# An encoder kernel: the latent heads' scores as three part products, and a new order of the work beside the heads

## The chip, the cores and the metric

The kernel runs on one core of a Trainium2 chip. Times are device microseconds from start to end of one execution. The core's engines run side by side, each through its own list of instructions in order: TensorE (PE; its weight loads are shown as PEld), VectorE (DVE), ScalarE (ACT), GpSimd (POOL) and SyncE (SP), which here only issues DMA transfers. Engines wait for each other through semaphores.

## The reference

Two layers of an encoder for 512 tokens of width 1024, float32. Each layer mixes tokens with three groups of heads, then attends to 256 memory tokens, then runs a gated feed-forward part. What matters here:

```python
a_q, a_k, a_v, b_cq, b_ckv, b_kr, c_q, c_k, c_v = split(rmsnorm(x, g_mix_pre[l]) @ w_in[l])
# latent heads: 4 heads, 64 plain + 32 rotated channels for q and k, 64 for v
qb = (rmsnorm(b_cq, mla_q_norm_g[l]) @ mla_w_q_up[l]).reshape(B, S, 4, 96)
qb = concat([qb[..., :64], rope(qb[..., 64:], positions)])
kvb = (rmsnorm(b_ckv, mla_kv_norm_g[l]) @ mla_w_kv_up[l]).reshape(B, S, 4, 128)
kb = concat([kvb[..., :64], broadcast(rope(b_kr, positions))])
s = einsum('bqhd,bshd->bhqs', qb, kb) / sqrt(96)         # the latent heads' scores
o_b = einsum('bhqs,bshd->bqhd', softmax(s), kvb[..., 64:])
o_a = diff_attention(...)   # 4 heads;  o_c = swa_attention(...)  # 8 heads, window of 128
x = x + rmsnorm(concat([o_a, o_b, o_c]) @ w_out[l], g_mix_post[l])
k, v = split(rmsnorm(mem, g_x_mem[l]) @ w_xkv[l])        # cross attention's keys, values
x = x + rmsnorm(attend(rmsnorm(x, g_x_pre[l]) @ w_xq[l], k, v) @ w_xo[l], g_x_post[l])
gate, up = split(rmsnorm(x, g_ffn_pre[l]) @ w_ffn_in[l])
x = x + rmsnorm((silu(gate) * up) @ w_ffn_out[l], g_ffn_post[l])
```

## The kernel before, in words

**Products.** A float32 operand is split into a high part (ScalarE casts it to float32r, L103) and a low part (VectorE subtracts the high part from it, L104). A product is then three float32r matmuls into one accumulator: high x high, high x low, low x high (`mm3`, L150 to L152). Two things stay plain float32: transposes (a matmul with the identity, L183, L416, L783) and the scores of the latent heads (L801). A plain float32 matmul shows as two records in the trace.

**The mix phase of a layer** is a list of 64 units in the order of the heads: 16 of the differential heads (units 0 to 15), 32 of the windowed heads (16 to 47), 16 of the latent heads (48 to 63). A unit goes through stages: scores (`score`), softmax (`soft`: VectorE finds the row's maximum, ScalarE exponentiates), transposes of the softmax (L416), splits of them (`ph`, `pl`), products with the values (L589, L590; accumulator `av`) and the eviction. At each step t of the list one stage of several units is emitted.

**Filling.** Between units, a generator `fill` emits other tensor work, as much per step as `FILL_PLAN` allows. Its order is: the rest of the projections into the heads; then the pieces that the string `FILL_ORDER` lists, one letter per piece; then the keys' rest, the values, and, from unit 48 on, the output projection (`out_first`, `early`, `out_late`). The letters are q, the windowed heads' second half of q; u, the latent heads' up-projection; m, the norm of the memory; k, the cross attention's keys (`make_xK`). The tile framework then schedules each engine's list from priorities and dependences, so the list that an engine runs can differ from the text's order.

**The up-projection** (`mla_up`) loads two weights, splits them, and goes over four tiles of 128 tokens. In `products` it multiplies the normed latents (`latT`) with the weights, copies, rotates (VectorE, L763 to L774) and writes the values `mV` (high on ScalarE, L424, low on VectorE, L425). In `transposed` it transposes q and k of four heads (L783) and ScalarE writes them, scaled, as float32 into `qT` and `kT` (L784). A letter u emits the transposes of the tile before and the products of the next.

**The memory's norm** (`mem_norm`) works on two tiles of 128 memory tokens, each in two halves: SyncE loads them into buffers named o, of which there are two (L1059); ScalarE squares and sums (L202); GpSimd makes the factor (L206, L207); VectorE scales in place (L223); TensorE transposes (L183); ScalarE and VectorE write high and low parts (`memTh`, `memTl`). Two letters m are one tile.

**Buffers.** Two accumulators (PSUM) for each of the names mm, sc, at, av; two staging buffers `st` for weights; eight pairs of split weights (`wh`, `wl`); named slots (Q0, Q1, D, E and others) that stages of a layer use one after the other. x0 to x3 hold the residual, 512 tokens; in the mix phase they hold the windowed heads' q (`SQ`: x0 and x1 for units 16 to 31, x2 and x3 for units 32 to 47), and the residual's tiles are loaded again at L1324.

SyncE issues all loads and stores in one queue, in order: one that waits for its buffer holds all behind it.

## Time and profile before

| what | us |
|---|---|
| median of 3 runs | 1575.53 (1573.16 to 1575.6) |
| profiled execution | 1577.2 |
| its span from first to last instruction | 1575.4 |
| TensorE matmuls / weight loads busy | 1539.2 / 1312.4 |
| VectorE, ScalarE, GpSimd busy | 980.2, 799.5, 93.7 |

Busy time is summed over instructions; weight loads lie beside matmuls, and the end of a matmul's record reaches over the start of the next. The trace's clock of TensorE is the granted share of full speed.

### The profile page before, as it was taken

The numbers are of one execution on the slowest core, as the hardware profiler recorded it, in microseconds if no ns is written. First come the engines' busy times: TensorE is split into PE (matmuls) and PEld (weight loads), VectorE is DVE, ScalarE is ACT, GpSimd is POOL, SyncE is SP. The second block draws the span as 40 slices with busy tenths as digits, with TensorE's granted clock in tenths as the row PEclk, the third lists the DMA queues.
The fourth block names the chain that finished last, engine by engine and source line by source line (L and its number), as shares of the span: only waits on it lengthen the run. The fifth ranks groups of instructions, "written<-read, shape, count | busy, mean of one in ns | idle before, by whom it ended". The sixth has DMA issues, their size and how long they took to land. (4 is left out here: it accounts for less than half of the span.)

```text
span 1575.4 us, 21922 instructions
## 1 busy us (share of the span) xinstructions
PE 1539.2 (98%) x8225; PEld 1312.4 (83%) x8225; DVE 980.2 (62%) x1927; ACT 799.5 (51%) x1741; POOL 93.7 (6%) x196
## 2 busy tenths in 40 slices
PE   6998999999999999999999999999999999999998
PEld 6987987899888888888888878778888888888886
DVE  6898877765653454454566988857546444445544
ACT  4588889544543233222356788875444532222321
POOL 2200000200100000000130000002002000000000
PEclk9999999999999999999999999999999999999999
DMA  5532551241243323232236135513303423233221
GB/s 179 161 95 88 188 164 56 81 161 54 81 134 109 105 84 104 81 116 98 89 125 148 51 125 177 167 41 107 127 36 110 144 81 107 80 108 107 80 81 54
DMA packets 130299, 168.69 MB, mean 107 GB/s; under 512 B 21776, under 2 KB 100752, under 8 KB 129424
## 3 DMA queue, kind: packets, MB, share of 16 engines
q1 hardware_dynamic: 130192, 167.28, 33.2%
q8 instruction: 65, 1.06, 0.3%
q14 instruction: 42, 0.34, 0.1%
HBM read 150.88 MB, written 10.09 MB: 102 GB/s over the span
## 5 line engine op out<-in xcount | busy, mean ns | idle before, releaser
L104 DVE TENSOR_TENSOR wl<-st,wh 128x512 fp32r<-128x512 f32 (+1 forms) x406 | 273.4, 686 | 245.1 <-ACT wh L103 244.4
L103 ACT CAST wh<-st 128x512 fp32r<-128x512 f32 (+1 forms) x406 | 243.7, 616 | 308.7 <-PE ps_mm L151 130.4
L152 PE MATMUL ps_mm<-hfh,wl 128*128 128x512 f32 (+1 forms) x384 | 142.8, 372 | 2.1 <-DVE wl L104 2.1
L150 PE MATMUL ps_av<-hfh,wh 128*128 128x512 f32 (+1 forms) x384 | 142.9, 372 | 0.0
L152 PE MATMUL ps_av<-hfh,wl 128*128 128x512 f32 (+1 forms) x384 | 142.6, 371 | 0.0
L150 PE MATMUL ps_mm<-hfh,wh 128*128 128x512 f32 (+1 forms) x384 | 142.6, 371 | 0.0
L151 PE MATMUL ps_mm<-hfl,wh 128*128 128x512 f32 (+1 forms) x384 | 142.6, 371 | 0.0
L151 PE MATMUL ps_av<-hfl,wh 128*128 128x512 f32 (+1 forms) x384 | 142.6, 371 | 0.0
L150 PE MATMUL ps_sc<-dwh,f 128*128 128x512 f32 x320 | 124.7, 390 | 0.0
L151 PE MATMUL ps_sc<-dwl,f 128*128 128x512 f32 x320 | 124.5, 389 | 0.0
L152 PE MATMUL ps_sc<-dwh,f 128*128 128x512 f32 x320 | 124.5, 389 | 0.0
L103 ACT CAST dwh<-st 128x1024 fp32r<-128x1024 f32 x40 | 40.1, 1050 | 157.5 <-PE ps_sc L152 153.6
L104 DVE TENSOR_TENSOR pl<-ps_at,ph 128x512 fp32r<-128x512 f32 (+1 forms) x128 | 82.7, 654 | 24.5 <-ACT ph L103 23.4
L152 PEld LDWEIGHTS ps_mm<-hfh,wl 128*128 128x128 f32 x384 | 72.3, 188 | 14.9 <-DVE wl L104 2.5
L151 PEld LDWEIGHTS ps_mm<-hfl,wh 128*128 128x128 f32 x384 | 72.4, 189 | 12.5
L152 PEld LDWEIGHTS ps_av<-hfh,wl 128*128 128x128 f32 x384 | 72.3, 188 | 12.5
L150 PEld LDWEIGHTS ps_mm<-hfh,wh 128*128 128x128 f32 x384 | 72.3, 188 | 12.5
L151 PEld LDWEIGHTS ps_av<-hfl,wh 128*128 128x128 f32 x384 | 72.2, 188 | 12.5
L150 PEld LDWEIGHTS ps_av<-hfh,wh 128*128 128x128 f32 x384 | 72.3, 188 | 12.3
L103 ACT CAST ph<-ps_at 128x512 fp32r<-128x512 f32 (+1 forms) x128 | 70.4, 561 | 23.9 <-PE ps_at L416 22.9
L206 POOL TENSOR_SCALAR rpost<-rpostss 128x1 f32<-128x1 f32 x24 | 11.9, 496 | 1173.1 <-ACT hTh L202 703.7
L416 PE MATMUL ps_at<-ident,e 128*128 128x128 f32 x480 | 77.2, 275 | 3.7 <-DVE memTl L104 2.1
(363 smaller groups left out, 3849.6 us busy)
## 6 DMA issues: line engine op xcount, KB each, us to landing
st<-in_w_ffn_in SPq DMA_DIRECT2D x44, 1024.0 KB, 4.9
st<-in_w_ffn_out SPq DMA_DIRECT2D x22, 1024.0 KB, 4.8
st<-in_w_xkv SPq DMA_DIRECT2D x16, 1024.0 KB, 5.4
st<-in_w_out SPq DMA_DIRECT2D x16, 512.0 KB, 5.2
st<-in_w_xq SPq DMA_DIRECT2D x8, 1024.0 KB, 5.3
st<-in_w_xo SPq DMA_DIRECT2D x8, 1024.0 KB, 5.0
st<-in_w_in SPq DMA_DIRECT2D x12, 512.0 KB, 3.9
q<-stg SPq DMA_DIRECT2D x48, 128.0 KB, 2.3
```

The source lines that it names most:

```text
L103: cast = nc.scalar.copy(hi, src)
L104: nc.vector.tensor_tensor(out=lo, in0=src, in1=hi.bitcast(F32), op=ALU.subtract)
L150: nc.tensor.matmul(ps, lhsT=lh, rhs=rh, start=first, stop=False)
L151: nc.tensor.matmul(ps, lhsT=lh, rhs=rl, start=False, stop=False)
L152: nc.tensor.matmul(ps, lhsT=ll, rhs=rh, start=False, stop=last)
L206: nc.gpsimd.tensor_scalar(out=r, in0=ms[:, 0:1], scalar1=ms[:, 1:2], scalar2=EPS, op0=ALU.add, op1=ALU.add)
L416: nc.tensor.transpose(pt[:, c * P:(c + 1) * P], e[:, k * P:(k + 1) * P], ident)
```

## The change

The scores of the latent heads become `mm3`, so `qT` and `kT` are each written in a high and a low part. The q part is scaled while it is written, so its low part is a multiply and subtract (two VectorE instructions, for heads 0, 1 and for heads 2, 3, into the tiles x0 and x1); the high parts are in the slots Q0 and Q1, the low part of k is in slot E. The string FILL_ORDER now also lists the values (v), and three of four tiles of the up-projection come behind the keys. At the second u the generator holds until step 31, so that the slots which units 16 to 31 read are free. The values' accumulators, staging and products are unchanged.

```diff
--- before.py
+++ after.py
@@ -38,7 +38,7 @@
 TMP_BUFS = {"e": 5, "ph": 2, "pl": 2, "o": 2, "c": 2, "m": 3}
 PS_BUFS = {"mm": 2, "sc": 2, "at": 2, "av": 2}
 NORM = {"swa": ("act", "dve"), "mla": ("act", "act")}
-FILL_ORDER = "qqummummukkkuu"
+FILL_ORDER = "qqummmmkkkkkkkkuvuuvuvv"
 FILL_PLAN = ((16, 2.5), (32, 2.2), (48, 1.6), (64, 0.8))
 FILL_STEP = 0.4
 LAG = (3, 4, 3)
@@ -741,11 +741,13 @@
                 lambda b, k: cV[:, k, 2 * b:2 * b + 2, :].rearrange("p b d -> p (b d)"), [end])
 
 
-        def mla_up(qT, kT, mV):
+        def mla_up(mla):
             st = stage(((0, 0, 0, mla_w_q_up[l].rearrange("(k p) n -> p k n", p=P)),), 2, 384)
             uq = unit(st)
             st = stage(((0, 0, 0, mla_w_kv_up[l].unsqueeze(1)),), 1, S)
             ukv = unit(st)
+
+            mV = mla["V"]
 
             def products(i):
                 t0, t1 = i * P, (i + 1) * P
@@ -776,12 +778,23 @@
                 return qn, kn
 
             def transposed(i, qn, kn):
+                qT, kT = mla["qT"], mla["kT"]
                 t0, t1 = i * P, (i + 1) * P
-                for n, t, sc in ((qn, qT, 96.0 ** -0.5), (kn, kT, 1.0)):
+                for n in (qn, kn):
                     pt = psum("at")
                     for h in range(4):
                         nc.tensor.transpose(pt[0:96, h * P:(h + 1) * P], n[:, h, :], ident)
-                    nc.scalar.mul(t[:, :, t0:t1], pt[0:96].rearrange("p (h t) -> p h t", h=4), sc)
+                    ptv = pt[0:96].rearrange("p (h t) -> p h t", h=4)
+                    if n is kn:
+                        split(kT[0][:, :, t0:t1], kT[1][:, :, t0:t1], ptv)
+                        continue
+                    sc = 96.0 ** -0.5
+                    hi = qT[0][:, :, t0:t1]
+                    nc.scalar.mul(hi, ptv, sc)
+                    for j in range(2):
+                        nc.vector.scalar_tensor_tensor(
+                            out=qT[1][j][:, :, t0:t1], in0=ptv[:, 2 * j:2 * j + 2], scalar=sc,
+                            in1=hi[:, 2 * j:2 * j + 2].bitcast(F32), op0=ALU.mult, op1=ALU.subtract)
 
             pend = None
             for i in range(NT + 1):
@@ -798,8 +811,9 @@
                 if a == 0:
                     u["nm"], u["sm"] = small(2, "mnm"), small(2, "msm")
                 ps = u["s"][a] = psum("sc")
-                nc.tensor.matmul(ps, lhsT=mla["qT"][:, h, i * P:(i + 1) * P], rhs=mla["kT"][:, h, :],
-                                 start=True, stop=True)
+                (qh, ql), k = mla["q"](h), mla["k"](h)
+                t_ = slice(i * P, (i + 1) * P)
+                mm3(ps, qh[:, t_], ql[:, t_], *k, True, True)
                 nc.vector.tensor_reduce(out=u["nm"][:, a:a + 1], in_=ps, axis=AX.X, op=ALU.max, negate=True)
 
             def soft(u, a, hi_):
@@ -813,7 +827,7 @@
 
             return chunk_units(
                 score, soft, [[((hh, i), (hh, i + 1), 0, NT) for i in (0, 2)] for hh in range(2)],
-                lambda hh, k: mla["mV"][:, k, c, 2 * hh:2 * hh + 2, :].rearrange("p b d -> p (b d)"),
+                lambda hh, k: mla["V"][:, k, c, 2 * hh:2 * hh + 2, :].rearrange("p b d -> p (b d)"),
                 [chunk_out(lambda: mdst(2 + c))])
 
 
@@ -873,22 +887,26 @@
                     head.settle()
                 yield
             qs = in_swa_q(1)
-            mla["qT"] = slot("Q0", [96, 4, S], F32, "qT")
-            mla["kT"] = slot("Q1", [96, 4, S], F32, "kT")
-            mla["mV"] = slot("D", [P, NT, 2, 4, 64], F32R, "mV")
-            ups = mla_up(mla["qT"], mla["kT"], mla["mV"])
             memT, mem_gen = mem_norm(l)
             xk = make_xK(l, memT)
-            steps = {"u": ups, "q": qs, "m": mem_gen, "k": xk}
+            steps = {"q": qs, "m": mem_gen, "k": xk, "v": make_xV(l, memT)}
             for g in FILL_ORDER:
+                if g == "u" and "k" not in mla and "u" in steps:
+                    yield 31
+                    qT = slot("Q0", [96, 4, S], F32R, "qTh"), [xp.tile([96, 2, S], F32R, tag=f"x{j}", name=f"qTl{j}")
+                                                               for j in range(2)]
+                    kT = slot("Q1", [96, 4, S], F32R, "kTh"), slot("E", [96, 4, S], F32R, "kTl")
+                    mla.update(qT=qT, kT=kT, q=lambda h: (qT[0][:, h], qT[1][h // 2][:, h % 2]),
+                               k=lambda h: (kT[0][:, h], kT[1][:, h]))
+                elif g == "u" and "u" not in steps:
+                    mla["V"] = slot("D", [P, NT, 2, 4, 64], F32R, "mV")
+                    steps["u"] = mla_up(mla)
                 next(steps[g])
                 yield
-            run_all(qs, mem_gen, ups)
+            run_all(*steps.values())
             mla["ready"] = True
-            yield from xk
             acc = slot("Sq", [P, NT, 512], F32, "acc")
             accs = state["acc"] = [acc[:, i, :] for i in range(NT)]
-            yield from make_xV(l, memT)
             yield 48 + most
             yield from out_first(w_out[l], mT, accs)
             early()
```

TensorE's list in layer 0 around the memory's second tile, first in the kernel before (L183 with `o` are the memory's transposes; `latT` and L783 belong to the up-projection; `memTh` to the keys):

```order
L183 MATMUL ps_at<-ident,o 128x128 x8
L416 MATMUL ps_at<-ident,e 128x128 x4
L589 MATMUL ps_av<-ph,KScV 128x256
L783 MATMUL ps_at<-ident,m 96x128 x8
L590 MATMUL ps_av<-pl,KScV 128x256
L589 MATMUL ps_av<-ph,KScV 128x256
L590 MATMUL ps_av<-pl,KScV 128x256
L705 MATMUL ps_sc<-KScV,SQ_555 128x256
L706 MATMUL ps_sc<-KScV,SQ_555 128x256
L705 MATMUL ps_sc<-KScV,SQ_554 128x384
L706 MATMUL ps_sc<-KScV,SQ_554 128x384
L150 MATMUL ps_mm<-wh,latT 128x384
```

The list goes on with eight more products of `latT`, the memory's other eight transposes in two groups of four, and eight transposes of L783. The same place in the changed kernel, up to the first products of the keys:

```order
L183 MATMUL ps_at<-ident,o 128x128 x8
L416 MATMUL ps_at<-ident,e 128x128 x4
L589 MATMUL ps_av<-ph,KScV 128x256
L590 MATMUL ps_av<-pl,KScV 128x256
L589 MATMUL ps_av<-ph,KScV 128x256
L590 MATMUL ps_av<-pl,KScV 128x256
L705 MATMUL ps_sc<-KScV,SQ_555 128x256
L706 MATMUL ps_sc<-KScV,SQ_555 128x256
L183 MATMUL ps_at<-ident,o 128x128 x8
L150 MATMUL ps_mm<-memTh_1507,wh 128x256 x2
L151 MATMUL ps_mm<-memTl_1508,wh 128x256
L152 MATMUL ps_mm<-memTh_1507,wl 128x256
```

The products of `latT` and the transposes L783 are no longer between the memory's two groups of transposes; they stand behind the keys.

VectorE's list at a tile of the up-projection, in the kernel before (L766 to L774 are the rotation, L425 the low part of the values; `pl` and L708 belong to the windowed heads' softmax):

```order
L766 TENSOR_TENSOR m<-m,sin_128 128x5x16
L572 TENSOR_SCALAR e<-e,sr 128x384
L768 TENSOR_TENSOR m<-m,sin_128 128x5x16
L708 ISA e,snm<-ps_sc,swd,nsinks 128x256
L708 ISA snm 128x1
L771 TENSOR_TENSOR m<-m,cos_127 128x160
L104 TENSOR_TENSOR wl<-st,wh 128x512
L425 TENSOR_TENSOR mV<-ps_mm,mV 128x2x128
L773 TENSOR_TENSOR m<-m 128x4x32
L774 TENSOR_TENSOR m<-m 128x4x32
```

The same engine at such a tile in the changed kernel, beside the values' projection (lines are two higher there):

```order
L572 TENSOR_SCALAR e<-e,sr 128x256
L795 SCALAR_TENSOR_TENSOR qTl_2432<-ps_at,qTh 96x2x128
L795 SCALAR_TENSOR_TENSOR qTl_2433<-ps_at,qTh 96x2x128
L765 COPY m<-kr 128x32
L104 TENSOR_TENSOR kTl<-ps_at,kTh 96x4x128
L768 TENSOR_TENSOR m<-m,sin_128 128x5x16
L770 TENSOR_TENSOR m<-m,sin_128 128x5x16
L708 ISA e,snm<-ps_sc,swd,nsinks 128x384
L708 ISA snm 128x1
L773 TENSOR_TENSOR m<-m,cos_127 128x160
L721 TENSOR_TENSOR esink<-snm,sinks 128x2
```

Three instructions per tile are added (`qTl` twice, `kTl`), in the same list as the softmax of the windowed heads and the low parts of weights.

SyncE's list before the output projection, in the kernel before (`x` are the residual's tiles):

```order
L1079 DMA xK_dram<-o 128x512
L1324 DMA x_3692<-in_x 128x1024
L112 DMA st<-in_w_xkv 128x4x512
L1324 DMA x_3693<-in_x 128x1024
L1079 DMA xK_dram<-o 128x512
```

And in the changed kernel, where those two loads are issued now:

```order
L112 DMA st<-in_w_xq 128x8x256
L112 DMA st<-in_w_out 128x2x512
L1342 DMA x_3739<-in_x 128x1024
L112 DMA st<-in_w_out 128x2x512
L1342 DMA x_3740<-in_x 128x1024
L112 DMA st<-in_w_out 64x4x512 x2
```

The loads of the residual's first two tiles have moved from the keys' stretch to between the loads of the output projection's weights.

## Rows read from the trace of the kernel before

**Rows 1.** The page's first part: busy us (share of the span), instructions

```profile
PE 1539.2 (98%) x8225; PEld 1312.4 (83%) x8225; DVE 980.2 (62%) x1927; ACT 799.5 (51%) x1741; POOL 93.7 (6%) x196
```

**Rows 2.** Busy time by stretches, three of layer 0, one of layer 1

```profile
core 0: us, PE busy (x) PEld busy (x) DVE busy (x) ACT busy (x) POOL busy (x), PEclk, DMA share, GB/s
131.50:156.50 25.00, 19.88 (x105) 15.65 (x104) 20.30 (x60) 20.61 (x53) 1.07 (x3) 0.86 0.32 105
156.50:229.00 72.50, 72.48 (x492) 65.39 (x492) 59.79 (x174) 59.84 (x154) 2.15 (x1) 1.00 0.51 162
229.00:262.00 33.00, 32.80 (x166) 22.59 (x165) 28.09 (x61) 32.42 (x76) 0.00 (x0) 1.00 0.37 114
...
1003.00:1039.00 36.00, 34.57 (x180) 24.47 (x179) 28.95 (x63) 34.10 (x78) 0.00 (x0) 1.00 0.36 124
```

**Rows 3.** The latent scores: shortest, median, longest ns, first and last start

```profile
L801 PE MATMUL ps_sc<-kT,qT x64: 590/592/697, 232.6 to 1047.4; 96*128 96x512 f32 x64
```

**Rows 4.** Timeline of TensorE in the latent stage: start us, us, instruction

```profile
249.79 1.88 PE L801 MATMUL ps_sc<-kT,qT 96*128 96x512 f32 x4
...
265.16 0.39 PE L150 MATMUL ps_mm<-wh,mixT 128*128 128x512 f32 x1
265.39 0.39 PE L151 MATMUL ps_mm<-wl,mixT 128*128 128x512 f32 x1
...
268.79 1.02 PE L801 MATMUL ps_sc<-kT,qT 96*128 96x512 f32 x2
...
270.56 1.02 PE L801 MATMUL ps_sc<-kT,qT 96*128 96x512 f32 x2
```

**Rows 5.** Timeline of layer 0 at the memory's norm, all engines

```profile
141.27 1.35 PE L183 MATMUL ps_at<-ident,o 128*128 128x128 f32 x8 [0.60 <-DVE sr L725]
...
141.97 1.07 SPq L1059 DMA_DIRECT2D o<-in_mem  x2
...
147.01 0.56 POOL L207 TENSOR_TENSOR rmem<-rmem,neghalf 128x1 f32<-128x1 f32 x1
...
147.29 0.56 PE L590 MATMUL ps_av<-pl,KScV 128*128 128x256 f32 x1
...
147.61 0.75 DVE L223 SCALAR_TENSOR_TENSOR o<-o,rmem,gains 128x512 f32<-128x512 f32 x1
...
148.76 0.75 DVE L223 SCALAR_TENSOR_TENSOR o<-o,rmem,gains 128x512 f32<-128x512 f32 x1
...
152.60 0.60 PE L783 MATMUL ps_at<-ident,m 128*96 128x128 f32 x4
...
154.04 0.38 PE L150 MATMUL ps_mm<-memTh,wh 128*128 128x256 f32 x1
```

**Rows 6.** Stretches of one us at the same place

```profile
144.00:145.00 1.00, 0.62 (x4) 0.22 (x2) 0.89 (x2) 0.79 (x2) 0.00 (x0) 0.54 0.75 262
150.00:151.00 1.00, 1.00 (x6) 1.00 (x6) 0.07 (x1) 0.07 (x1) 0.00 (x0) 0.55 0.00 0
151.00:152.00 1.00, 1.00 (x9) 0.96 (x8) 0.45 (x1) 1.00 (x4) 0.00 (x0) 1.00 0.00 0
```

**Rows 7.** Timeline of layer 1 at the memory's norm

```profile
924.28 0.75 DVE L223 SCALAR_TENSOR_TENSOR o<-o,rmem,gains 128x512 f32<-128x512 f32 x1 [0.85 <-POOL rmem L207]
...
925.25 0.75 DVE L223 SCALAR_TENSOR_TENSOR o<-o,rmem,gains 128x512 f32<-128x512 f32 x1
...
929.48 0.39 PE L150 MATMUL ps_mm<-memTh,wh 128*128 128x256 f32 x1
```

**Rows 8.** VectorE's groups by shape: busy us, mean ns

```profile
L104 DVE TENSOR_TENSOR pl<-ps_at,ph 128x512 fp32r<-128x512 f32 x112 | 76.4, 688 | 24.5 <-ACT ph L103 23.4
...
L425 DVE TENSOR_TENSOR mV<-ps_mm,mV 128x256 fp32r<-128x256 f32 x8 | 3.3, 418 | 0.4 <-ACT mV L424 0.4
```

**Rows 9.** Timeline: issue of output weights, and ScalarE's wait for them

```profile
267.72 8.43 SPq L112 DMA_DIRECT2D st<-in_w_out  x3
...
282.47 2.18 ACT L103 CAST wh<-st 128x512 fp32r<-128x512 f32 x4 [0.68 <-DMA st<-in_w_out]
```

## The prediction

> **What bounds the kernel now.** The page's busy shares come first [rows 1]: TensorE is busy 1539.2 of 1575.4 us, so time is won only where TensorE does less or waits less. What it is worth differs by stage, so the table by stretches comes next [rows 2]. From 156.5 to 229 us, where the cross attention's keys and values are projected beside the windowed heads, TensorE is busy 72.48 of 72.5 us, while VectorE and ScalarE are busy 59.8: tensor work decides, with 12.7 us of vector time left over. From 229 to 262 us, where the latent heads run, ScalarE is busy 32.42 of 33 us and its matmuls' records cover 32.80: two engines are full, and ScalarE has 0.58 us to give. In layer 1 the same stage, 1003 to 1039 us, has ScalarE at 34.10 of 36. From 131.5 to 156.5 us TensorE is busy only 19.88 of 25 us and at a mean clock of 0.86: there it waits on a chain, the memory's norm. Those three places are what the change touches.
>
> **The change, part 1: the scores.** 32 plain float32 products (64 records, two per product) go [rows 3]. In a run of four records, 1.88 us with the last one's 0.59 inside, the starts stand (1.88 - 0.59) / 3 = 0.43 us apart [rows 3, 4], so one product holds TensorE for 0.86 us. A three-part product of the same 512 columns is three matmuls whose starts stand 0.23 us apart (265.16, 265.39) [rows 4], 0.68 us in all. Each score gives back 0.175 us, 32 of them 5.6 us. Passed on is only what ScalarE can follow. Before 262 us it can give 0.58 us; the two scores behind it (268.79 and 270.56, two records each [rows 4]) pass their 0.35 us whole. In layer 1 ScalarE has 36 - 34.10 = 1.90 us, and two scores stand late there as well, 0.35. Sum 0.58 + 0.35 + 1.90 + 0.35 = **-3.2 us**, with bounds 0 and -5.6.
>
> Here a rule of the Trainium skill speaks to the same row. The trace's row says that matmuls cover 32.80 of 33 us and weight loads 22.59, 68%, against 65.39 of 72.5, 90%, in the dense stretch [rows 2]. The Trainium skill, "Perfetto Trace Analysis", section "Identifying the Most-Contended Engine", holds that matmul busy time is a poor measure of nearness to the limit since matmuls are pipelined, and that the weight loads' share is a good one. By that rule TensorE has slack in this stage and a saving there may come to nothing; by the matmul share all 5.6 us would come.
>
> **Part 2: the memory's norm loses its cover.** Before, the up-projection of the latent heads is woven between the norm's steps; now three of its four tiles come only behind the keys. The norm is a chain: the first memory tile's transposes at 141.27 free the buffers, the second tile's two loads are issued at 141.97, ScalarE squares its halves, GpSimd ends the factor at 147.57, VectorE scales from 147.61 and again from 148.76 (in between it does short steps of the up-projection), and the first key product starts at 154.04 [rows 5]. On TensorE's own list this stretch held 16 transposes and 9 products of the up-projection; now it holds about 2.5 us of other work between the two groups of memory transposes, and behind them the keys at once. Without those steps the second scaling ends at 147.61 + 2 x 0.75 = 149.11, the last four transposes take 0.6 more, and the keys can start at 149.7: 4.3 us sooner than before. The work that moves behind them at full speed: a group of four transposes lasts 0.60 [rows 5], 16 about 2; nine products at 0.23 for 512 columns and about 0.18 for the shorter ones another 2: 4.0 us (3.5 to 4.2). If nothing else changed, layer 0 would gain 0.3. But the granted clock is half at 144 to 145 and still 0.55 at 150 to 151, when TensorE had been working without a pause since 147.29, and full from 151 on [rows 5, 6]. Before, those 3.6 us of half speed were beside the chain's waiting; now TensorE is emptier ahead of the keys, so half speed reaches into them, and half of 3.6 us is 1.8 us lost at most, none at least. I take 1.25, since the stretch is emptier than the one that lost the clock before. Layer 0: -4.3 + 4.0 + 1.25 = +0.95. Layer 1: the second scaling stands at 925.25 behind 924.28 with one short step between, the first key product at 929.48 [rows 7]; without it the scaling ends at 925.78, the keys start at 926.4, 3.1 us sooner: -3.1 + 4.0 + 1.25 = +2.15. Sum **+3.1 us**; bounds -0.4 (no clock lost, 3.5 moved) and +4.6 (1.8 lost each, 4.2 moved).
>
> **Part 3: the vector queue in the values' stretch.** Each tile of the up-projection now writes its low parts: two VectorE instructions of 96 x 256 for q, one of 96 x 512 for k. The nearest rows are 0.418 us for 256 columns and 0.688 us for 512 [rows 8], so 1.5 to 1.6 us per tile and 6.4 us per layer. ScalarE's two instructions per tile stay of their length. These tiles, with their old vector instructions of about 1.9 us each, now stand beside the values' projection, whose 96 products at 0.23 are 22 us of TensorE. VectorE is free there 17.5% of the time [rows 2], 4 us, and would take 3 x 1.9 + 6.4 = 12 us more in that part, while the keys' part gets 5.7 us back. Splits of weights stand in the same vector queue, so TensorE could wait for a low part of a weight or of a softmax; weight splits run ahead of use and absorb much of it, and the windowed heads' work can shift. Per layer between -0.5 (a lighter keys' part) and +4; I take +1, nearer the low end, because over the whole 72.5 us the 12.7 us free cover the 6.4: **+2 us** together.
>
> **Part 4: loads.** The low parts of q sit in the buffers into which the residual's first two tiles are loaded again. Before, those loads were issued in the keys' and values' stretch; now they stand in SyncE's queue between the output projection's weight loads and wait for the last scores of two heads each. Behind them are queued the weights whose casts wait at 282.47 for 0.68 us [rows 9]. The last loads of that group are issued three in a run from 267.72, 8.43 us long [rows 9], so the third starts only some 7 us later than the first, behind the last score at 270.56: the release of a weight buffer, not the new wait, comes last. I take **0**; each layer up to +1 if the wait comes last.
>
> **Sum**: -3.2 + 3.1 + 2.0 + 0 = +1.9 us. The profiled execution took 1577.2 us, 1.8 beyond its span; it would become 1579.1. It stands 1.7 us above the median of the runs shown, 1575.53, so the forecast against that median is 1577.4.
>
> **Rivals.** *The scores' saving comes whole.* ScalarE's load in the latent stage is movable too (casts of weights and evictions could come earlier or later), and products of the output projection may fill what is left. Then -5.6; with no clock lost the norm costs -4.3 + 4.0 - 3.1 + 4.0 = +0.6, and the vector queue nothing: -5.0, so 1570.5. For it: VectorE and ScalarE have 12 us free in the dense stretch; against it: ScalarE's 98% [rows 2].
>
> *Slower: VectorE's queue decides in the values' stretch.* If the 12 us land on 4 free ones and TensorE waits for half the excess, each layer loses 4 us: -3.2 + 3.1 + 8 = +7.9, 1583.4. It decides from the point where VectorE's work in that stretch exceeds TensorE's, that is, if under half of the 8 us of excess can shift. For it: the order of the new instructions, in which the low parts of four tiles stand close together among the softmax's instructions. Against it: the eight buffers of split weights.
>
> *It doesn't do what it says: the scores' saving comes to nothing.* ScalarE's list in the latent stage is unchanged, so TensorE ends each product sooner and waits longer for the next softmax: 0 + 3.1 + 2.0 = +5.1, 1580.6. This is what the weight loads' share of 68% would mean [rows 2]. The Trainium skill's rule on that share, named above, would forecast this case.
>
> **How the numbers follow.** About 0.2%, 3.15 us, is what a measurement of this kernel can tell from no change: below 1572.4 is faster, above 1578.7 slower. The forecast's own range is 1573 to 1580.5, chance 0.46 (0.34 of it no measurable change, 0.12 slower). The saving whole, 1570.5: 0.28 (0.24 faster, 0.04 same). The vector queue, 1583.4: 0.17, all slower. The saving swallowed, 1580.6: 0.09 (0.03 same, 0.06 slower). Together faster 0.24, same 0.41, slower 0.35. The range, which leaves a tenth on either side, starts below the first rival at 1568 and ends above the second at 1586; all bounds at once would give -0.4 - 5.6 - 1 = -7.0 (1568.5) and 0 + 4.6 + 8 + 2 = +14.6 (1590), which needs four mishaps in one run and is left out.
>
> **What would show it.** Scores: matmul starts of 0.23 us in the latent stage, and ScalarE still 98% busy, with the stage shorter by about 1 us in layer 0 and 2 in layer 1. Norm: keys starting near 149.7 and 926.4, with a granted clock below 0.6 in the first microseconds of the keys. Vector queue: TensorE's waits for low parts of weights, softmax or q and k in the values' stretch, together about 1 us per layer. Loads: the residual's first two loads issued near 262 and 271 without a longer wait of ScalarE for the output weights. It is wrong if the latent stage shortens by the whole 2.8 us per layer, if the clock never falls at the norm, or if TensorE waits over 2 us per layer for VectorE.

## The result, and the profile after

The changed kernel took 1589.57 us (median of four runs, 1589.26 to 1591.08), the kernel before 1574.46 beside it (four runs, 1573.16 to 1575.6): a ratio of 1.0095, 95% interval 1.0083 to 1.0107. It is slower, and 3.6 us above the upper end of the forecast's range. The profiled execution took 1589.26 with a span of 1587.2, 11.8 us longer than the span before; the medians differ by 15.1 us, mainly because the profiled execution of the kernel before, 1577.2, lies 2.7 us above its median. Readings against its trace can come out too small by that much.

The page's first part of the changed kernel, which answers to [rows 1] (busy us, share of the span, instructions):

```profile
PE 1544.8 (97%) x8257; PEld 1320.5 (83%) x8257; DVE 992.4 (63%) x1951; ACT 800.6 (50%) x1741; POOL 91.7 (6%) x196
```

The busy totals say little: VectorE has 12.2 us more (the low parts), TensorE 5.6 more, though less is multiplied. The span grew by 11.8, so TensorE also waits 6.2 us more in sum. To see where, I put the two timelines side by side at events that both have. In this text N is the start of the memory's first transposes, S the first latent score, X the first score of the cross attention.

| stretch | before, layer 0 / 1 | after, layer 0 / 1 | difference |
|---|---|---|---|
| N to S: norm, keys, values | 91.30 / 88.53 | 97.89 / 96.21 | +6.59 / +7.68 |
| S to X: latent heads, output projection | 107.09 / 109.51 | 107.87 / 107.87 | +0.78 / -1.64 |
| X of layer 0 to N of layer 1 | 578.35 | 578.31 | 0 |
| X of layer 1 to the end | 459.34 | 459.45 | +0.1 |

Layer 0's N comes 1.7 us earlier in the profiled execution of the changed kernel, which with these differences makes the 11.8. (N stands between 139.6 and 141.3 us in kernels that are alike up to there, so that is a spread between executions.) So the whole loss of 14.3 us lies between the memory's norm and the latent stage, and the stretch from S to X, for which the scores were made cheaper, gives back 0.9. The order has a part in that stretch too: with the new order and plain scores (e1 below) it takes 108.55 and 110.42 us, so against that kernel the cheaper scores give back 0.68 and 2.55, together 3.2.

Stretches of the changed kernel (us from:to, length, busy us of each engine with its instructions, granted clock, DMA share, GB/s): the norm, the keys, the gap between the last key product and the first value product, the values, the latent stage, all in layer 0, then gap and values of layer 1:

```profile
139.60:149.80 10.20, 6.17 (x27) 4.49 (x27) 7.27 (x15) 6.31 (x15) 1.26 (x2) 0.65 0.16 51
149.80:183.50 33.70, 33.70 (x259) 32.37 (x259) 27.66 (x72) 25.71 (x64) 2.03 (x1) 0.95 0.48 149
183.50:192.50 9.00, 7.57 (x47) 5.98 (x46) 6.93 (x25) 7.19 (x22) 0.00 (x0) 1.00 0.45 146
192.50:233.70 41.20, 40.56 (x223) 33.66 (x224) 35.05 (x110) 32.97 (x87) 0.00 (x0) 1.00 0.29 84
237.50:284.60 47.10, 47.08 (x270) 39.38 (x269) 33.95 (x67) 42.11 (x92) 0.00 (x0) 1.00 0.39 127
...
965.90:974.90 9.00, 7.60 (x47) 6.00 (x46) 7.02 (x25) 7.18 (x22) 0.00 (x0) 1.00 0.47 147
974.90:1016.10 41.20, 40.56 (x223) 33.67 (x224) 35.08 (x110) 33.00 (x87) 0.00 (x0) 1.00 0.28 84
```

Keys, gap and values of layer 0 in the kernel before:

```profile
154.00:193.60 39.60, 38.91 (x306) 36.55 (x306) 35.24 (x102) 34.38 (x87) 2.15 (x1) 1.00 0.51 167
193.60:194.90 1.30, 1.30 (x14) 1.30 (x13) 1.22 (x7) 1.13 (x4) 0.00 (x0) 1.00 0.92 370
194.90:226.50 31.60, 31.58 (x170) 26.44 (x169) 23.30 (x71) 24.34 (x66) 0.00 (x0) 1.00 0.44 126
```

Three things are to be seen. The keys went from 39.6 to 33.7 us, since the windowed heads' stages and the up-projection beside them went elsewhere. A gap of 9.0 us stands where there were 1.3, with TensorE idle 1.43 us in it. And the values went from 31.6 to 41.2 us, with 53 matmuls more and VectorE at 85% instead of 74%. The two layers agree to 0.1 us, so this is built into the order and is no accident of one execution.

The gap, from TensorE's timeline of the changed kernel (start us, us, instruction, idle time before it and its releaser), at the last key product and the first value product:

```profile
183.45 0.28 PE L152 MATMUL ps_mm<-memTh,wl 128*128 128x256 f32 x1
...
188.80 0.39 PE L705 MATMUL ps_sc<-KScV,SQ 128*128 128x256 f32 x1 [0.32 <-DVE snm L708]
...
190.28 0.66 PE L416 MATMUL ps_at<-ident,e 128*128 128x128 f32 x4 [0.38 <-ACT e L570]
...
191.84 0.38 PE L589 MATMUL ps_av<-ph,KScV 128*128 128x256 f32 x1 [0.47 <-ACT ph L103]
192.48 0.50 PE L150 MATMUL ps_mm<-wh,memTh 128*128 128x512 f32 x1 [0.26 <-ACT m L764]
```

Here TensorE waits in turn for four steps of the windowed heads and of the up-projection. With no filling at hand the latency of each step shows. The code says why: counted by the amounts in FILL_PLAN, the keys' last piece is emitted at step 28 and the next piece, a tile of the up-projection, would be due at step 30; the hold puts it off to step 31, and it is the only tile between the keys and the values.

The norm, which answers to [rows 5] and [rows 6] (one-microsecond stretches, and TensorE's timeline):

```profile
143.00:144.00 1.00, 0.69 (x4) 0.29 (x2) 0.75 (x2) 0.21 (x1) 0.00 (x0) 0.50 0.33 127
...
152.00:153.00 1.00, 1.00 (x6) 1.00 (x6) 1.00 (x3) 0.93 (x3) 0.00 (x0) 0.52 0.00 0
153.00:154.00 1.00, 1.00 (x11) 1.00 (x10) 0.97 (x2) 0.62 (x1) 0.00 (x0) 1.00 0.00 0
```

```profile
147.98 1.94 PE L183 MATMUL ps_at<-ident,o 128*128 128x128 f32 x8 [1.39 <-DVE o L223]
149.79 0.80 PE L150 MATMUL ps_mm<-memTh,wh 128*128 128x256 f32 x2
...
152.18 0.41 PE L152 MATMUL ps_mm<-memTh,wl 128*128 128x256 f32 x1
152.39 0.41 PE L150 MATMUL ps_mm<-memTh,wh 128*128 128x256 f32 x1
```

The keys start at 149.79, and the first of them follow each other 0.21 us apart (152.18, 152.39) instead of 0.12 (183.33, 183.45 at the end of the keys), at a granted clock of 0.5, 1.2 of 2.4 GHz. The mean of 0.52 from 152 to 153 puts the rise at the end of that microsecond, when TensorE had worked without a pause since 147.98.

The latent stage, which answers to [rows 4], at its first two scores:

```profile
237.49 0.40 PE L150 MATMUL ps_sc<-kTh,qTh 96*128 96x512 f32 x1
...
238.19 0.39 PE L150 MATMUL ps_sc<-kTh,qTh 96*128 96x512 f32 x1
```

A score now holds TensorE for 238.19 - 237.49 = 0.70 us instead of 0.86. The new instructions of VectorE (both layers; busy us, mean ns, idle time before them):

```profile
L795 DVE SCALAR_TENSOR_TENSOR qTl<-ps_at,qTh 96x256 fp32r<-96x256 f32 x16 | 6.1, 413 | 0.9 <-ACT qTh L793 0.9
...
L104 DVE TENSOR_TENSOR kTl<-ps_at,kTh 96x512 fp32r<-96x512 f32 x8 | 5.5, 684 | 0.7 <-ACT kTh L103 0.5
```

### The profile page after: what moved, and what is told of

It is laid out like the page before. It is cut to its first block, busy times and chain, and to the rows that moved or that the text cites. A ratio compares the mean times of both kernels' runs of the same rounds, so it can differ in the third digit from the quotient of the medians.

```text
span 1587.2 us, 22008 instructions
## 1 busy us (share of the span) xinstructions
PE 1544.8 (97%) x8257; PEld 1320.5 (83%) x8257; DVE 992.4 (63%) x1951; ACT 800.6 (50%) x1741; POOL 91.7 (6%) x196
## 4 chain that ended last, share of the span: by engine, by line
PE 44%; DVE 2%; ACT 2%; POOL 1%; issue 1%; DMA 0%; DVEq 0%; POOLq 0%; ACTq 0%; SPq 0%
PE ps_mm L150 7%; PE ps_mm L152 7%; PE ps_mm L151 7%; PE ps_sc L150 3%; PE ps_av L151 3%; PE ps_av L150 3%; PE ps_sc L152 3%; PE ps_sc L151 3%; PE ps_av L152 3%; PE ps_at L416 2%; PE ps_av L589 1%; PE ps_av L590 1%; PE ps_sc L638 1%; DVE x L238 0%; PE ps_at L183 0%
```

## The experiments

Every ratio is to runs of the kernel before on the same chip. It is not the ratio of the two medians: for g1, whose seven runs spread from 1577.87 to 1586.66 us, the medians alone would give 1.0021.

| kernel | scores | order | median us | ratio (95%) |
|---|---|---|---|---|
| after | three parts | new | 1589.57 | 1.0095 (1.0083 to 1.0107) |
| e3 | three parts | new, loads by GpSimd | 1590.25 | 1.0100 (1.0085 to 1.0115) |
| e1 | plain | new | 1594.55 | 1.0119 (1.0104 to 1.0134) |
| e2 | plain | new, no hold | 1589.79 | 1.0089 (1.0072 to 1.0106) |
| eB | plain | no hold, tiles in the keys | 1581.97 | 1.0045 (1.0030 to 1.0060) |
| eA | plain | no hold, norm covered, two tiles beside the values | 1577.57 | 1.0018 (1.0009 to 1.0027) |
| f3 | three parts | new, no hold | 1585.02 | 1.0069 (1.0052 to 1.0086) |
| f4 | three parts | no hold, tiles in the keys | 1579.19 | 1.0028 (1.0016 to 1.0040) |
| e8 | three parts | old, one tile later | 1581.12 | 1.0036 (1.0026 to 1.0045) |
| g1 | three parts | old | 1578.45 | 1.0036 (1.0021 to 1.0051) |
| e5 | high parts only, three matmuls | old | 1576.68 | 1.0010 (1.0001 to 1.0020) |
| e6 | high parts only, one matmul | old | 1576.86 | 1.0009 (0.9999 to 1.0019) |
| f1 | plain, ScalarE relieved | old | 1575.05 | 1.0003 (0.9994 to 1.0012) |
| f2 | e5, ScalarE relieved | old | 1567.51 | 0.9957 (0.9942 to 0.9971) |
| g2 | g1, ScalarE relieved | old | 1581.50 | 1.0040 (1.0028 to 1.0052) |
| g3 | g1, relieved twice as much | old | 1579.32 | 1.0031 (1.0021 to 1.0042) |
| g4 | after, ScalarE relieved | new | 1588.41 | 1.0086 (1.0073 to 1.0099) |
| g6 | g1, rotation on GpSimd | old | 1574.06 | 0.9998 (0.9989 to 1.0007) |
| g7 | g6, ScalarE relieved | old | 1572.91 | 0.9987 (0.9979 to 0.9996) |

**The change taken apart: order or scores?** e1 keeps the new order with the hold and returns to plain float32 scores; e2 is e1 without the hold; e8 has the three-part scores in the old order, save one tile of the up-projection.

```diff
 # e1, against after (score)
-                mm3(ps, qh[:, t_], ql[:, t_], *k, True, True)
+                nc.tensor.matmul(ps, lhsT=mla["qT"][:, h, i * P:(i + 1) * P], rhs=mla["kT"][:, h, :], start=True, stop=True)
 # e2, against e1
-                    yield 31
 # e8, against before: mm3, low part of k in slot E, of q in slot H3, from there by ScalarE to x0, x1
-FILL_ORDER = "qqummummukkkuu"
+FILL_ORDER = "qqummmumukkkuu"
```

> The changed kernel with the scores as plain float32 again: no low parts of q and k, no use of x0 and x1, the residual's loads free again. The new order of pieces and the hold until step 31 stay. Theory A, the order costs (the memory's norm without cover, the hold that leaves a stretch without filling): it loses the scores' saving of 3 to 6 us and keeps most of the loss, so 1584 to 1592 us. Theory B, the low parts cost (vector queue in the values' stretch, late residual loads): 1575 to 1579 us.

> As the run before, but the up-projection is not held until step 31, which plain scores don't need. If the hold costs what the trace shows as idle TensorE between the last key product and the first value product (2.6 us a layer), this is 4 to 6 us below the run before. If the idle time there only moves, they agree within 2 us.

> Three-part scores with real low parts in nearly the old order (only the third step of the memory's norm comes ahead of the second up-projection piece). The low part of q is kept in the slot H3 until step 32 and then copied by ScalarE to x0 and x1. Theory A: the scores' saving without the order's cost, 1568 to 1573 us. Theory B: low parts cost 2 us or more per layer and the residual's loads stay late, 1576 to 1582 us.

The order alone made the kernel 1.19% slower, more than the whole change did. The three-part scores, which cost 0.36% in the old order (e8, and g1 below), are worth about a quarter per cent in the new one (after against e1, whose intervals just touch; f3 against e2 and f4 against eB show 0.20 and 0.17%). The theory that the low parts on VectorE's queue are the main loss falls here: e1 has none of them.

**The order, step by step.** eA and eB are e2 with other strings: eB brings the tiles of the up-projection back beside the keys and leaves the norm bare; eA covers the norm again and leaves the last two tiles behind the keys, beside the values. f3 is the changed kernel without the hold (the low part of q then needs a place of its own, and ScalarE copies it to x0 and x1 after the list), f4 is f3 with eB's order.

```diff
 # after, e1, e2, f3
 FILL_ORDER = "qqummmmkkkkkkkkuvuuvuvv"
 # eB, f4
+FILL_ORDER = "qqummmukukukukkkkkvvvv"
 # eA
+FILL_ORDER = "qqummummukkkkkkkkuvuvvv"
 # f3, against after; qTl in slot H3, written by one instruction
-                    yield 31
 ...
+            yield 32
+            for h in range(4):
+                nc.scalar.copy(mla["qx"][h // 2][:, h % 2, :], mla["qT"][1][:, h, :].bitcast(F32))
```

> Plain float32 scores, no hold; the memory's norm is woven with the up-projection as in the kernel before, and only the last two tiles stand behind the keys, beside the values. Against the plain scores in the new order without hold (1589.8) it gives the norm its cover back. If the bare norm is most of the order's 14 us: 1577 to 1581. If the values' stretch is: 1585 to 1589.

> Plain float32 scores, no hold; the memory's norm runs without the up-projection's tiles as in the changed kernel, but the tiles are spread over the keys and none stands beside the values. If the bare norm is most of the order's 14 us: 1585 to 1590. If the values' stretch is: 1577 to 1581. Sum of this run's and the other one's losses over the kernel before should be near 14 us if the two are independent.

> The changed kernel without the hold until step 31: the low part of q is written to the slot H3 as soon as its tile is there, and ScalarE copies it to x0 and x1 once the windowed heads have left them. Everything else as changed. If the hold's price with plain scores (4.8 us) holds here too: 1584 to 1586. If the vector work of the low parts only takes its place: 1588 to 1590.

> As the run before, but the tiles of the up-projection are spread over the keys instead of the values; the memory's norm stays bare. If placing the tiles beside the values is what costs (plain scores: 7.8 us): 1577 to 1580. If the low parts cost wherever they stand: 1584 or more.

Each step back is seen. Without the hold: 1.0095 to 1.0069 with three parts, 1.0119 to 1.0089 with plain scores. Tiles away from the values: 1.0069 to 1.0028, and 1.0089 to 1.0045. What is left in eB, 0.45% or 7.1 us (interval 4.7 to 9.4), is the price of the bare norm with plain scores, as far as eB isolates it (its tiles also stand a little otherwise among the keys); eA, with the norm covered and two tiles beside the values, stands at 1.0018. With three parts covering the norm shows no gain (f4 1.0028, g1 1.0036). The gap between keys and values and the values' own stretch, first of f3, then of f4:

```profile
183.50:189.20 5.70, 5.62 (x43) 5.17 (x41) 5.20 (x17) 4.78 (x15) 0.00 (x0) 1.00 0.74 229
189.20:229.90 40.70, 40.26 (x224) 33.58 (x223) 34.88 (x110) 36.31 (x95) 0.00 (x0) 1.00 0.32 90
```

```profile
193.70:195.00 1.30, 1.30 (x13) 1.30 (x12) 0.90 (x3) 1.30 (x4) 0.00 (x0) 1.00 1.01 377
195.00:227.00 32.00, 31.42 (x169) 26.46 (x168) 24.96 (x77) 25.90 (x69) 0.00 (x0) 1.00 0.43 125
```

Without the hold the gap is 5.7 us, with TensorE full in it; with the tiles beside the keys it is 1.3 again and the values take 32.0 us. That part of the work now stands in the keys, so the lengths alone prove no loss. The loss is in N to S, over all of it: 97.89 / 96.21 (after), 96.14 / 94.30 (f3), 92.34 / 92.69 (f4), against 91.30 / 88.53 before. The same tiles cost 3.8 and 1.6 us more beside the values than beside the keys. Not all of that is waiting: between N and S the trace of f3 has 9 matmuls more than that of f4 in each layer (581 and 576 against 572 and 567). The medians of f3 and f4 differ by 5.8 us. The low parts are not needed for it: plain scores give the same step, 0.44% (e2, eB). In e2, with plain scores, the values' stretch looks like after's, with VectorE at 80%:

```profile
191.20:232.30 41.10, 40.56 (x222) 33.43 (x221) 33.08 (x104) 35.28 (x92) 0.00 (x0) 1.00 0.36 109
```

Which wait it is stays open. In this stretch of after and of e2 ScalarE is 80% and 86% busy and VectorE 85% and 80%, the matmuls stand a tenth of a microsecond late again and again, and no single releaser holds most of it. Single traces carry this no further, because the clock differs between them: from N to S e1 takes 97.41 / 98.42 and e2, without the hold, 97.44 / 96.15, though the medians differ by 4.8 us; in the trace of e2 TensorE stood at half clock from 138.6 to 155.5 in layer 0, in that of e1 from 144.3 to 151.

**The late loads.** e3 takes the loads of the residual's first two tiles out of SyncE's queue.

```diff
-            nc.sync.dma_start(xt[i], ...)
+            (nc.gpsimd if i < 2 else nc.sync).dma_start(xt[i], ...)
```

> The changed kernel with the residual's first two loads issued from GpSimd's queue, so that SyncE's queue no longer waits in front of the output weights. If those waits cost (the step put at 0 in the forecast, the rival of late weights says 2 us a layer): 4 us below the changed kernel, 1585.5. If they are hidden: within 1.5 us of 1589.5.

No change (1.0100 against 1.0095), so the waiting loads hold nothing up. SyncE's timeline of the changed kernel shows them between the output weights, as the program's order had it:

```profile
253.81 0.34 SPq L1342 DMA_DIRECT2D x<-in_x  x1
272.55 0.37 SPq L112 DMA_DIRECT2D st<-in_w_out  x1
275.09 0.34 SPq L1342 DMA_DIRECT2D x<-in_x  x1
280.37 1.27 SPq L112 DMA_DIRECT2D st<-in_w_out  x2
```

**What cheaper scores are worth.** e5 and e6 keep the old order and all else of the kernel before, and write q and k as float32r: three matmuls on the high parts, or one; the low parts are left out.

```diff
-                nc.tensor.matmul(ps, lhsT=mla["qT"][:, h, i * P:(i + 1) * P], rhs=mla["kT"][:, h, :], ...)
+                mm3(ps, q_, q_, k_, k_, True, True)                              # e5
+                nc.tensor.matmul(ps, lhsT=q_, rhs=k_, start=True, stop=True)     # e6
```

> The kernel before in its own order, with each score as three products of the high parts alone; the low parts are left out, so the scores are not the reference's. It is the tensor side of the change without its vector work and its order. If ScalarE swallows part, as forecast: 3.2 us below the kernel before, 1571. If all comes through: 5.6 below, 1569. If the saving is swallowed: 1574 to 1575.

> The kernel before in its own order with each score as one product of the high parts, a third of the tensor work of the run with three; the scores are not the reference's. It takes 14.6 us more of TensorE away (32 x 2 x 0.2275). Theory: the latent stage and the tail behind it are set by ScalarE and the residual's norm chain, so it ends within 5 us of the run with three products, 1572 to 1577. Rival: TensorE sets the stage and the lost saving was an accident of order, 1560 to 1565.

Neither gains, although e6 takes 32 x (0.86 - 0.23) = 20 us from TensorE. The latent stage of e5, then of e6:

```profile
230.80:266.30 35.50, 35.48 (x209) 29.33 (x208) 27.70 (x56) 34.86 (x79) 0.00 (x0) 1.00 0.24 83
```

```profile
230.40:263.90 33.50, 32.88 (x191) 26.16 (x190) 26.75 (x54) 32.76 (x75) 0.00 (x0) 1.00 0.25 81
```

ScalarE is 98% busy in both. What TensorE saves turns up as waits behind the stage, in the output projection and the norm after it. First e6, then e5, then the kernel before, whose longest wait from 262 us to X in layer 0 is 0.16:

```profile
275.25 0.74 PE L150 MATMUL ps_mm<-wh,mixT 128*128 128x512 f32 x2 [1.88 <-ACT wh L103]
...
301.36 0.66 PE L183 MATMUL ps_at<-ident,o 128*128 128x128 f32 x4 [1.14 <-DVE o L223]
```

```profile
310.61 0.63 PE L183 MATMUL ps_at<-ident,o 128*128 128x128 f32 x4 [1.11 <-DVE o L223]
314.55 0.39 PE L152 MATMUL ps_av<-hxh,wl 128*128 128x256 f32 x1 [0.98 <-DVE wl L104]
```

```profile
305.15 1.25 PE L183 MATMUL ps_at<-ident,c 128*128 128x128 f32 x8 [0.16 <-DVE hxl L104]
```

**ScalarE relieved.** f1, f2, g2 and g4 give a quarter of the latent softmax's scalings from ScalarE to VectorE, on before, e5, g1 and after; g3 gives half of them on g1.

```diff
 # f1, f2, g2, g4
-                        scaled(NORM["mla"][j], e, r[:, j:j + 1])
+                        scaled("dve" if j and hi_[1] == 3 else NORM["mla"][j], e, r[:, j:j + 1])
 # g3
+NORM = {"swa": ("act", "dve"), "mla": ("act", "dve")}
```

> The kernel before, with a quarter of the latent heads' scalings of the softmax moved from ScalarE to VectorE (8 of 32 per layer, 5.4 us of ScalarE's work). If ScalarE sets the latent stage, TensorE's plain scores beside it: faster by 1 to 3 us, 1572 to 1574. If TensorE sets it, or the tail behind takes it: within 1 us of the kernel before.

> The run with three products of the high parts in the old order (scores not the reference's), with the same quarter of the scalings on VectorE. If ScalarE swallowed the scores' saving: 3 to 6 us below that run, 1571 to 1574. If the output projection and the residual's norm behind the latent stage give it back, as in the run with one product: within 1.5 us of 1576.7.

The relief alone gains nothing (1.0003), the cheap product alone nothing (1.0010); together they gain 7.4 us (0.9957). The tail of f2 has none of e5's waits; from S to X it takes 104.32 / 105.24, where e5 takes 109.20 / 108.78 and the kernel before 107.09 / 109.51:

```profile
299.67 1.25 PE L183 MATMUL ps_at<-ident,c 128*128 128x128 f32 x8 [0.15 <-DVE hxl L104]
317.20 0.39 PE L151 MATMUL ps_mm<-hxl,q 128*128 128x256 f32 x1 [0.16 <-DVE hxl L104]
```

**With real low parts.** g1 is e8 with the string of the kernel before (the low part of q in slot H1).

> Three-part scores with real low parts in exactly the old order of pieces: the low part of k in the slot E, that of q in H1, copied by ScalarE to x0 and x1 at step 32. Against the run with high parts only (1576.7) it adds the vector work of the low parts. If that is hidden beside the keys: 1575.5 to 1578. If it costs 2 us or more a layer: above 1580.

> The run before with a quarter of the latent heads' scalings moved from ScalarE to VectorE. If ScalarE is what swallowed the scores' saving: 7 to 9 us below the run before, 1567 to 1570, below the kernel before. If the low parts and the copies refill the engines: 1573 to 1577.

> The same with half of the scalings on VectorE (16 of 32 per layer). VectorE was busy 28 of 33 us in the latent stage; 8 us more fill it. If the gain is ScalarE's alone, it is as fast as with a quarter or faster; if VectorE becomes the bound, it is 2 to 5 us slower than with a quarter.

> The changed kernel itself with a quarter of the scalings on VectorE. Its latent stage is 47.1 us against 48.6 and 51.0 before. If ScalarE holds it, 4 to 8 us below the changed kernel, 1582 to 1586; if its late weights and the tail hold it, within 2 us of 1589.5.

With real low parts the relief is worth nothing that can be measured: 1.0040 and 1.0031 against 1.0036 in the old order, and 1.0086 against 1.0095, with overlapping intervals, in the new one. From N to S g1 takes 94.46 / 91.67, 3 us more per layer than before, and from S to X 106.45 / 107.84, 2.3 less in both together: in the old order the low parts cost more than the cheaper scores give back. The trace, of an execution 3.5 us above the median, has most of the loss beside the keys, not in the norm: the first key product comes 12.80 and 12.00 us behind N, before 12.77 and 11.47; the keys behind it take 42.5 us in layer 0 (rows below), before 39.6. Why g2, with the relief, shows nothing of what f2 gained stays open.

**A version that gives the loss back.** If VectorE's work beside the keys is the price of the low parts, other work must leave it. g6 is g1 with the six small operations of the rotation (L763 to L774, the copy shown and five tensor_tensor) on GpSimd, which the page shows busy 6% of the time; g7 is g6 with the relief of ScalarE.

```diff
-                nc.vector.tensor_copy(out=r5[:, 4, :], in_=kr[:, i, :])
+                nc.gpsimd.tensor_copy(out=r5[:, 4, :], in_=kr[:, i, :])
...
```

> Real low parts in the old order (1578.5), with the rotation of q and k (six small vector instructions a tile, about 1.5 us) on GpSimd. If VectorE's load beside the keys is what the low parts cost: 3 to 6 us less, 1573 to 1576. If the longer GpSimd steps stretch each tile's chain by as much: 1578 or more.

> The run before with a quarter of the latent heads' scalings on VectorE. If both loads were the causes: 1568 to 1572, below both kernels. If the tail behind the latent stage gives it back as with real low parts and ScalarE work alone: 1575 or more.

g6 takes back the 0.36% of g1 (0.9998). g7 gains a little (0.9987, interval 0.9979 to 0.9996): 1.9 us below the kernel before, 16.7 below the changed one, with the three-part scores in full. Its interval overlaps that of g6, so the relief is not shown to add anything. The kernel before with its rotation on GpSimd and plain scores was not run; how much of this the three-part scores bring is therefore not shown. The keys of g1, then of g6:

```profile
154.00:196.50 42.50, 41.56 (x309) 38.56 (x310) 36.43 (x104) 33.15 (x87) 2.15 (x1) 0.96 0.38 119
```

```profile
153.10:191.20 38.10, 38.10 (x306) 36.27 (x304) 34.43 (x91) 34.00 (x89) 8.39 (x12) 1.00 0.47 158
```

For about as many matmuls the keys take 4.4 us less, and TensorE no longer waits in them (busy 41.56 of 42.50 in g1, 38.10 of 38.10 in g6). Part of it is the clock: a mean of 0.96 over 42.5 us is 3.4 us at half speed, some 1.7 us lost, and g6 has 1.00 there.

## Why the prediction was wrong

**What bounds the kernel.** Right for the latent stage, where ScalarE is as full as TensorE. Incomplete in the dense stretch, of which it said that tensor work decides with 12.7 us of vector time left over [rows 2]. That was read in the old order, in which the gap between keys and values is 1.3 us and full; the forecast took that one number for a new order in which the same work lies in other places.

**Part 1, the scores.** -3.2 foreseen, and about right in size when each kernel is read against plain scores in the same order, from S to X: -3.2 (after, e1), -2.2 (f3, e2), -2.9 (f4, eB), -2.3 (g1, before). The -0.9 of the changed kernel against the kernel before has the order's own loss in it. By the timed ratios, the work of the low parts included, three parts gain 0.24, 0.20 and 0.17% in the three new orders, 3.8 to 2.7 us. In the old order they lose: g1 by 0.36%, and e5 and e6, which have no low parts, gain nothing. There the count stopped too early: it took 0.58 and 1.90 us as gained once TensorE was through the scores, and e5 and e6 lose them again in waits of the output projection and the norm behind it. That only what ScalarE can follow is passed on is shown by f1, e5 and f2, for kernels without low parts: either limit alone holds the time. The rival that the saving is swallowed, at 0.09, holds for e5 and e6 but not for the changed kernel. The Trainium skill's rule that the forecast weighed there ("Perfetto Trace Analysis", "Identifying the Most-Contended Engine"), that weight loads and not matmuls tell how near TensorE is to its limit, agrees with e6: at a share of 68% [rows 2], 20 us of matmul time could be taken away for nothing. It does not agree with f1 and f2: with ScalarE relieved the cheaper products gain 7.4 us, and without them the relief gains none, so TensorE was a limit too.

**Part 2, the norm.** Right in mechanism, too small in size by the timed ratio. The keys come sooner and start at half clock. From N to the first key product layer 0 takes 149.79 - 139.60 = 10.19 us, where 149.7 - 141.27 = 8.43 was foreseen, and 12.77 before: 2.6 us sooner, not 4.3. The clock's term was 1.25 us per layer; in layer 0 TensorE worked at half speed for 5.0 us without a pause, 2.5 lost. Foreseen were +3.1 in all, with +4.6 as the most. eB against the kernel before shows +0.41 and +2.94 from N to S, together +3.35, which looks like a hit; but the timed ratio says 7.1 us (4.7 to 9.4), and 1.8 us more are lost from S to X in layer 1. The agreement of the first sum is luck: the trace of the kernel before is of an execution at a mean clock of 0.995, while its executions lie between 0.995 and 0.999 and those of eB between 0.992 and 0.994. With three parts no gain of the cover is seen (f4 and g1): g1 loses beside the keys instead, and why is not shown.

**Part 3, the vector queue.** Here a step of the working failed. +2 was taken for the low parts and the move of the three tiles together. The move alone, with no low part in it, costs 0.44% (e2 against eB, plain scores) and 0.41% with three parts (f3 against f4): 6.9 and 6.5 us. The forecast said that the old vector instructions of the tiles "now stand beside the values' projection", counted 12 us on 4 free ones, and then took +1 per layer since "over the whole 72.5 us the 12.7 us free cover the 6.4". The free time beside the keys did not help the values. The rival in which this queue decides, at 4 us per layer, had the right place and nearly the size; it was given 0.17. That VectorE is what the values wait for, as it says, is not shown. What the low parts cost by themselves is not settled either: three parts against plain scores from N to S show +1.85 (f4, eB), +6.3 (g1, before), but -1.7 (after, e1) and -3.2 (f3, e2), in traces whose clocks differ.

**What the sum did not hold.** The hold until step 31. The front of the document tells of it, but it has no term: it stands at nothing without a reason. e1 and e2 differ by this one line, and the times by 0.30%, 4.7 us; after and f3 differ by 0.26%, 4.1 us, though f3 also writes and copies the low part of q in another way. Without the hold the time, 1585.02 in f3, is inside the range; it would also be inside without the loss of the tiles.

**Part 4, the loads.** Right: 0 foreseen, and e3 shows no cost. They were issued at 253.81 and 275.09, where 262 and 271 were foreseen.

The timed ratios give the account with plain scores: bare norm 0.45%, tiles beside the values 0.44%, hold 0.30%, three parts -0.24% (after against e1). They add up to the 0.95% of the changed kernel because each is the step from one kernel to the next, so the sum proves nothing by itself; but the first two steps are clear of their intervals, and in the third no run of one kernel comes within 2 us of the other. Foreseen for the order, low parts included, were 3.1 + 2.0 + 0 = 5.1 us; the order alone took 1.19%, 18.7 us. The time is close to the 1590 of all upper bounds together, but not by the four mishaps named there: the loads cost nothing, the norm went past its bound, and the hold was in no bound.

## What to carry to other kernels

When work is moved from one stretch to another, price it in the stretch that receives it, not by the free time of both, and look at what the generator emits while it holds: here one step's delay of one tile cost 0.3%. To price one part of a change, read it against a kernel that has the other parts, not against the kernel before. Where two engines are full in the same stage, an edit that relieves one of them may bring nothing until the other is relieved too, as in f1, e5 and f2; follow the gain past the stage's end before counting it.

## What the runs showed of the hardware

In layer 0 of the changed kernel TensorE's clock stayed at 1.2 GHz for 5.0 us of uninterrupted work (147.98 to 152.95) behind the norm's pauses, of which half, some 2.5 us, is what full speed would have saved. The forecast took 1.25 and had 1.8 as the most, from the half speed of the kernel before (144 to 151); here it lasts from 143 to 153.

The mean granted clock differs between executions of one kernel, and the time goes with it. Of 89 executions of the kernel before, the 24 at 0.999 took 1573.7 us in the median and the 14 at 0.995 took 1576.1. The changed kernel's four stand at 0.992 to 0.994.

The six small operations of the rotation cost GpSimd about twice as much as VectorE, 22.8 us against 12.1 in both layers together, and were still well placed there. Two of them in g6, both layers:

```profile
L766 POOL TENSOR_TENSOR m<-m,sin 128x80 f32<-128x80 f32 x8 | 5.3, 662 | 11.3 <-ACT m L762 10.1 <-ACT esink L722 1.2
L771 POOL TENSOR_TENSOR m<-m,cos 128x160 f32<-128x160 f32 x8 | 4.6, 569 | 0.6
```

On VectorE, in g1, the same lines take 230 and 315 ns.
